# Another order of sections and blocks in z, three products instead of two in attention V, and maxima by transfer

## The chip, the cores and the metric

The kernel runs on one core of a Trainium2 chip. The metric is the device time of one execution in microseconds (us), the median of three runs. A core has TensorE (PE, matrix products, into PSUM), VectorE (DVE), ScalarE (ACT), GpSimd (POOL) and SyncE (SP), which here issues nearly all transfers (DMA). Each engine takes its instructions in a fixed order and waits on semaphores.

## The reference, cut to what matters

Two layers over 2048 latent and 256 context tokens of width 1024. In each, one input projection gives the columns of three head groups: a gMLP with spatial gating inside chunks of 128 (a_u, a_v, a_g), grouped-query attention with 8 heads of 64 and 2 key heads (q, k, v, b_g), and a bidirectional RG-LRU (r_x, r_g). The three results, gated, go through the output projection, a residual and a LayerNorm.

```python
z = (x * (1 + scale[:, None]) + shift[:, None]) @ w_in
a_u, a_v, a_g, q, k, v, b_g, r_x, r_g = jnp.split(z, IN_OFFSETS, -1)
q = axial_rope(rms_norm(q, q_norm_g), rows, cols)      # k likewise
attn = blocked_attention(q, concat([k, kc]), concat([v, vc]))   # softmax over 2304 keys
mix_a = chunk_gmlp(a_u, a_v, a_norm_g, a_norm_b, a_ws, a_bs)
xr = centred_dwconv(r_x, conv_w, conv_b)
lru = h_f + h_b                                        # one scan in each direction
y = concat([mix_a * silu(a_g), attn * silu(b_g), lru * silu(r_g)], -1) @ w_o
x_new = layer_norm(ALPHA * x + gate[:, None] * y, ln_g, ln_b)
```

In the last layer the context tokens need only what the latent tokens read of them (k, v and the LRU's state).

## The kernel before

A layer is a z phase and an attention phase. Both cut the tokens into nine blocks of 256: block 0 is the context, blocks 1 to 8 the latent tokens. Operands are split into a high and a low part in fp16, so that most products are sums of three.

**The z phase** (`z_phase`). A block's input is transposed and modulated by `prep` (PE tr, ACT xm, POOL xh, DVE xl). Then sections are run for the block, each a group of columns of the projection: rx and rg (LRU, products named cps), ag, kv, uv, bg (products named zps), in the order of the tuple `run`. A section's evacuations are ACT and DVE work out of PSUM. Longer follow-ups are generators: `lru` (convolution on DVE up to xrh and xrl, then the gate products gps on PE), `heads` (norm and rope of q and k on DVE and POOL, transposes kp and qp on PE, stores of QS), `gmlp` (products ga, transpose yt). `start` puts one into a list, and each `tick` of a section takes every one on to its next `yield`; so the yields set where a follow-up's PE work stands between the sections. Only PE's order is written out by hand in this phase; the other engines' is set by the scheduler. `rest` (`ada_rest`, the remaining adaLN vectors: products gtp, transposes gtr) and `fm` (`first_max`, the maxima of attention's first unit, products zms) are pumped between products inside a section. The last two blocks are woven by hand. PSUM banks are shared by tags: zc (cps, gps), tr (tr, kp, qp, yt, gtr, zms; two banks), zps (four banks).

**The attention phase** (`att_phase`). A unit is a block and a head, 136 in all (72 and 64). Its keys come in steps of 256: nine steps in a latent unit, one in a context unit, 1160 steps in all. A step has four score products of 256 columns (stp, two for each key tile: KK times QS, then KB times QB), ACT's exponential into P, a subtraction that gives the low part Pl (on POOL, now and then on DVE, by the costs that `use` adds up), and four steps later (LAG) the products with V (`attend`). Row 64 of QB holds the negated maximum of each query, so that the score comes out shifted. That maximum is made two to three units ahead: `max_chunks` (ten score products sps of 512 or 256 columns, reduced by DVE into pm, then mz), paced by `pace`; three steps behind the last chunk `row_out` calls `max_row`. At fixed rates the steps also take along the out-projection (wo: groups of three products wops of 512 columns, 32 groups a block in 17 blocks), its LayerNorm, the backward scan and the loading of weights. The order of PE, DVE, ACT and POOL is written out by hand here; SP's is the scheduler's.

Of the kernel before, what the change touches and what calls it, by code (L numbers as in the profile page):

```python
# [20 lines left out]
KC = 8  # L21
# [34 lines left out]
def tile_hybrid_groups(  # L56
# [23 lines left out]
    MZ = [cst.tile([128, 2, 65], F16, name=f"MZ{i}") for i in range(3)]  # L80
# [6 lines left out]
    def consts_late():  # L87
        V.memset(nhalf, -0.5)
        V.tensor_copy(idH, idF)
        V.memset(VX[:, :, :, 128:129], 1.0)  # L90
        for m in MZ:
            V.memset(m, 0.0)
        G.memset(KB[64:65], 1.0)
# [162 lines left out]
    def layer(l):  # L256
# [15 lines left out]
        def z_phase():  # L272
# [33 lines left out]
            def ada_rest():  # L306
                items = [(l2, j, k) for l2, j in [(0, 2)] + [(a, b) for a in range(1, DEPTH) for b in (2, 1, 0)]
                         for k in range(KC)]
                zer = MZ[1][:, 0, 0:1].to_broadcast([128, 128])
                mov = MZ[2][:, 0:1, 0:64].to_broadcast([128, 4, 64])  # L310
# [7 lines left out]
                def fin(l2, j, row):  # L318
# [13 lines left out]
                for i, (l2, j, k) in enumerate(items):  # L332
                    if k == 0:
                        acc = pp.tile([128, 256], F32, name="gtp", tag="zps", bufs=4)
# [12 lines left out]
                    if k == KC - 1:  # L347
                        V.tensor_tensor(row, acc, row, op=OP.add)
                        fins = l2, j, row
# [11 lines left out]
            def lru(b):  # L361
# [15 lines left out]
                yield  # L377
                rr = zp.tile([128, 2, 2, n], F32, name="gt0", tag="gt0")
# [58 lines left out]
            IW = 1.0 / WS  # L437
            xT = {}
# [13 lines left out]
            def prep(b):  # L452
# [4 lines left out]
                def xload(h):  # L457
                    for t in range(2):
                        xt = zp.tile([128, 512], F32, name="xn", tag="xn", bufs=4 if l == 0 else 2)
                        nc.sync.dma_start(xt, src[t * 128:(t + 1) * 128, h * 512:(h + 1) * 512])  # L460
                        xn[t, h] = xt
# [26 lines left out]
            def nat(xT_b, t, g, c0=0):  # L488
# [5 lines left out]
                for k in range(KC):  # L494
# [3 lines left out]
                    if t:  # L498
                        pump(fm, 1)
# [46 lines left out]
            def heads(b, qk, ss):  # L546
# [50 lines left out]
                yield  # L597
                for t in range(2):
# [20 lines left out]
            def first_max(QS):  # L619
# [11 lines left out]
                V.tensor_reduce(MZ[0][:, :, 64], zm, axis=AX, op=OP.max, negate=True)  # L631

            def sections(b, bi):
# [19 lines left out]
                def sec_rx():  # L653
# [13 lines left out]
                    if b >= 2 and (bi != 2 or full(0)):  # L667
# [3 lines left out]
                def sec_rg():  # L671
                    sg = zp.tile([128, 2, n], F32, name="sg", tag="sbg")
# [19 lines left out]
                def sec_kv():  # L692
                    pump(late, 100)
                    h0 = 0 if full(b) else 8
                    for t in range(2):
# [12 lines left out]
                        tick()  # L708
                    hd.append(heads(b, qk, ss))
# [14 lines left out]
                def sec_bg():  # L724
                    for t in range(2):
                        sbg = zp.tile([128, 512], F32, name="sbg", tag="th" if t and b < NB - 1 and (full(0) or bi != 2) else "sbg")
# [10 lines left out]
            def queue(*bis):  # L737
# [5 lines left out]
                start(chain())  # L743

            border = list(range(NB)) if full(0) else [1, 0] + list(range(2, NB))
            with tc.manual_schedule(engines={nc.tensor.engine}):
# [16 lines left out]
                for bi, b in enumerate(border):  # L763
# [26 lines left out]
        def att_phase():  # L790
# [8 lines left out]
            p = Router(op, ["aQS aQB", "P Pl", "asb wad brow pxn pxm pm ol rc", "yB yt aya ayc", "OH OL",  # L799
# [107 lines left out]
            blk, sbs, yas = {}, {}, {}  # L907
# [20 lines left out]
            def max_chunks(u):  # L928
# [4 lines left out]
                mz = MZ[u % 3]  # L933
                for t in range(2):
                    pm = p.tile([128, 5], F32, name="pm", tag="pm", bufs=4)
                    i = 0
                    for k0 in range(0, nk, 512):
# [8 lines left out]
                        if k0 + 512 >= nk:  # L946
                            V.tensor_reduce(mz[:, t, 64:65], pm[:, :i], axis=AX, op=OP.max, negate=True)
# [3 lines left out]
            def max_row(u):  # L951
                b, h = units[u]
                mz = MZ[u % 3]
# [85 lines left out]
            def attend(u, j):  # L1039
# [3 lines left out]
                if j == 0:  # L1043
                    pvs[u] = pp.tile([128, 2, 130], F32, name="pv", tag="pv" if b else "sps", bufs=2 if b else 3)
# [16 lines left out]
            def head_out(u):  # L1061
                b, h = units[u]
                pv = pvs.pop(u)
                ol = p.tile([128, 2, 64], F32, name="ol", tag="ol", bufs=2)
                S.copy(ol, pv[:, :, 0:64])
                yield
# [5 lines left out]
                V.reciprocal(rc, pv[:, :, 128])  # L1072
                V.tensor_tensor(pv[:, :, 64:128], ol, pv[:, :, 64:128], op=OP.add)
                for t in range(2):
                    hs = slice(h * 64, (h + 1) * 64)
                    V.scalar_tensor_tensor(yB[:, t, hs], pv[:, t, 64:128], rc[:, t:t + 1], sb[:, t, hs],  # L1076
                                           op0=OP.mult, op1=OP.mult)
                use(DV, 0.85)
                if h == 7:
                    outs.append(mix_t(b))  # L1080

# [293 lines left out]
```

## Time and profile before

| | |
|---|---|
| median of 3 runs | 2864.6 us (2861.25 to 2867.11) |
| profiled execution, own time | 2865.65 us |
| its span, first to last instruction | 2863.9 us |
| mean granted TensorE clock | 0.982 of full |
| z of layer 0, attention of layer 0 | about 0 to 664 us, 664 to 1500 us |
| z of layer 1, attention of layer 1 | about 1500 to 2070 us, 2070 to 2864 us |

Everything below is of the profiled execution. The stages overlap a little, and the borders are those of the first and last products of each.

### The profile page before, as it was taken

The numbers are of one execution on the slowest core, as the hardware profiler recorded it, in microseconds if no ns is written. First come the engines' busy times: TensorE is split into PE (matmuls) and PEld (weight loads), VectorE is DVE, ScalarE is ACT, GpSimd is POOL, SyncE is SP. The second block draws the span as 40 slices with busy tenths as digits, with TensorE's granted clock in tenths as the row PEclk, the third lists the DMA queues.
The fourth block names the chain that finished last, engine by engine and source line by source line (L and its number), as shares of the span: only waits on it lengthen the run. The fifth ranks groups of instructions, "written<-read, shape, count | busy, mean of one in ns | idle before, by whom it ended". The sixth has DMA issues, their size and how long they took to land. (4 is left out here: it accounts for less than half of the span.)

```text
span 2863.9 us, 60755 instructions
## 1 busy us (share of the span) xinstructions
PE 2688.2 (94%) x24121; PEld 1816.1 (63%) x24121; DVE 2031.8 (71%) x4013; ACT 1341.6 (47%) x2513; POOL 1757.0 (61%) x1812
## 2 busy tenths in 40 slices
PE   7999999889999998999999999998899999999998
PEld 3555555546776776677764655564487777777775
DVE  5565554558998876777887565554699898777776
ACT  2444343345654444444543454444466454454442
POOL 3244443346987876677864244443499897777774
PEclk9999999999999999999999999999999999999999
DMA  8232222105222210211115111110322321111001
GB/s 292 87 103 94 87 91 83 58 35 175 68 83 87 77 42 24 75 49 53 49 53 161 53 60 52 52 65 36 121 76 72 93 93 38 49 53 39 30 31 45
DMA packets 113717, 213.61 MB, mean 75 GB/s; under 512 B 13396, under 2 KB 45016, under 8 KB 113432
## 3 DMA queue, kind: packets, MB, share of 16 engines
q1 hardware_dynamic: 111060, 208.84, 21.9%
q8 instruction: 189, 3.10, 0.5%
q10 hardware_dynamic: 2372, 0.89, 0.1%
q14 instruction: 96, 0.79, 0.1%
HBM read 147.54 MB, written 62.14 MB: 73 GB/s over the span
## 5 line engine op out<-in xcount | busy, mean ns | idle before, releaser
L1036 POOL TENSOR_TENSOR Pl<-P 128x512 f16<-128x512 f32 x1118 | 1197.8, 1089 | 310.9 <-ACT P L1029 304.9
L1029 ACT ACTIVATE P<-stp 128x512 f32<-128x512 f32 x1160 | 692.0, 598 | 754.9 <-PE stp L1026 713.2
L942 DVE TENSOR_REDUCE pm<-sps 128x1 f32<-128x256 f32 (+1 forms) x1276 | 777.1, 628 | 249.8 <-PE sps L940 246.5
L1026 PE MATMUL stp<-aQB,KB 65*128 65x256 f16 x2320 | 579.6, 275 | 2.7 <-ACT aQB L957 2.7
L1025 PE MATMUL stp<-aQS,KK 128*128 128x256 f16 x2320 | 577.4, 274 | 0.2
L1053 PE MATMUL pv<-VX,P 128*128 128x129 f16 x4640 | 557.7, 220 | 1.3 <-ACT aQB L957 0.8
L1055 PE MATMUL pv<-VX,Pl 128*128 128x65 f16 x4640 | 527.3, 193 | 1.5 <-POOL Pl L1036 0.9
L1055 PEld LDWEIGHTS <-Pl 128*128 128x128 f16 x4640 | 414.9, 97 | 121.6 <-POOL Pl L1036 3.2
L940 PE MATMUL sps<-KK,aQS 128*128 128x256 f16 (+1 forms) x1276 | 456.3, 359 | 36.6 <-DVE pm L942 26.7
L1053 PEld LDWEIGHTS <-P 128*128 128x128 bf16 x4640 | 430.4, 98 | 41.5 <-issue 25.4
L1025 PEld LDWEIGHTS <-KK 128*128 128x128 f16 x2320 | 229.6, 99 | 85.8 <-issue 21.9
L1026 PEld LDWEIGHTS <-KB 65*128 65x128 f16 x2320 | 227.8, 98 | 70.5 <-issue 1.3
L484 POOL TENSOR_SCALAR xh<-xm 128x512 f16<-128x512 f32 x68 | 44.6, 656 | 288.3 <-ACT xm L481 287.7
L495 PEld LDWEIGHTS <-xh 128*128 128x128 f16 x1040 | 102.5, 99 | 122.9 <-issue 17.8
L497 PEld LDWEIGHTS <-xl 128*128 128x128 f16 x1040 | 102.4, 98 | 123.1 <-issue 3.5
L496 PEld LDWEIGHTS <-xh 128*128 128x128 f16 x1040 | 102.5, 99 | 115.6 <-issue 9.5
L646 PE MATMUL cps<-xh,wh_cc 128*128 128x256 f16 x528 | 148.7, 282 | 3.3 <-POOL xh L484 2.9
L648 PE MATMUL cps<-xh,wl_cc 128*128 128x256 f16 x528 | 148.1, 280 | 3.3 <-DVE wl_cc L158 3.3
L647 PE MATMUL cps<-xl,wh_cc 128*128 128x256 f16 x528 | 148.4, 281 | 0.4 <-DVE xl L485 0.4
L940 PEld LDWEIGHTS <-aQS 128*128 128x128 f16 x1276 | 125.1, 98 | 16.8 <-issue 2.1
L397 POOL TENSOR_SCALAR gt<-gt,sp 128x256 f32<-128x256 f32 x72 | 43.9, 618 | 144.8 <-ACT gt L394 138.8
L719 ACT ACTIVATE uv<-uv 128x512 f32<-128x512 f32 x34 | 21.4, 630 | 208.0 <-DVE uv L718 208.0
(273 smaller groups left out, 5416.2 us busy)
## 6 DMA issues: line engine op xcount, KB each, us to landing
wf<-in_w_in_dram SPq DMA_DIRECT2D x64, 256.0 KB
wga<-in_w_ada_dram SPq DMA_DIRECT2D x32, 512.0 KB
lr<-LRd SPq DMA_DIRECT2D x32, 512.0 KB
SBd<-sbg SPq DMA_DIRECT2D x34, 256.0 KB
QSd<-QS SPq DMA_DIRECT2D x17, 512.0 KB
LRd<-gt SPq DMA_DIRECT2D x34, 256.0 KB
aQS<-QSd SPq DMA_DIRECT2D x17, 512.0 KB
asb<-SBd SPq DMA_DIRECT2D x17, 512.0 KB
```

The costliest lines, as they stand in the source:

```text
L495: T.matmul(ps[:, :w], xh[:, k, ts], wh[:, k, c0:], start=(k == 0), stop=False)
L646: T.matmul(ps, wh[:, k, cs], xh[:, k], start=(k == 0), stop=False)
L647: T.matmul(ps, wh[:, k, cs], xl[:, k], start=False, stop=False)
L648: T.matmul(ps, wl[:, k, cs], xh[:, k], start=False, stop=(k == KC - 1))
L940: T.matmul(ps[:, :w], QS[:, h, t * 128:(t + 1) * 128], KK[:, kv].rearrange("p a b -> p (a b)")[:, k0:k0 + w], start=True, stop=True)
L942: V.tensor_reduce(pm[:, i:i + 1], ps[:, :w], axis=AX, op=OP.max)
L1025: T.matmul(ps[:, i], KK[:, kv, kt], QS[:, h], start=True, stop=False)
L1026: T.matmul(ps[:, i], KB[:, kv, kt], QB[:, h], start=False, stop=True)
L1029: S.activation(P, ps, AF.Exp)
L1036: less_busy(0.8, 1.06, 0.8).tensor_tensor(Pl, P, Ph, op=OP.subtract)
L1053: T.matmul(pv[:, t, 0:129], Ph[:, i, ts], VX[:, kt, kv, 0:129], start=first, stop=False, skip_group_check=True)
L1055: T.matmul(pv[:, t, 64:129], Pl[:, i, ts], VX[:, kt, kv, 64:129], start=False, stop=end, skip_group_check=True)
```

## The change

In z:
- layer 0 runs bg ahead of uv; block 7 runs three sections (rx, rg, ag) in its own turn instead of four, and the last two blocks are woven as rx 8, kv 7, uv 7, ag 8, kv 8, bg 7, uv 8, rg 8, bg 8;
- lru of blocks 7 and 8 starts in that block's kv, ahead of its heads, instead of in the next block's rx (block 7) or behind kv and heads (block 8); lru has one more yield in layer 0 (blocks up to 6), heads one more in all blocks but the last;
- sg and the first sbg of block 8 are taken from tag xn, both sbg of block 7 from tag sbg; the last prep is led two steps forward; first_max is pumped in both halves of a section;
- the gtr transposes write the free part of gtp's bank instead of a bank of tag tr.

In attention:
- the product with the high part of P, 129 columns, becomes two of 65 and 64, so that V's two halves sum up in the same 65 columns of PSUM with the low part's product; the copy to ol and the addition of the halves go;
- the maximum goes from mz (128 partitions) into row 64 of QB by two transfers, where two products (mp) and a copy on ACT did it. `MZ`, its zeros and its use as a zero operand go; `zeros` takes the last.

```diff
-                        tp = pp.tile([128, KC, 2], F32, name="gtr", tag="tr", bufs=2)
...
-                        acc = pp.tile([128, 256], F32, name="gtp", tag="zps", bufs=4)
+                        bank = pp.tile([128, 512], F32, name="gtp", tag="zps", bufs=4)
+                        acc = bank[:, 0:256]
...
                 yield
                 yield
+                if l == 0 and b < NB - 2:
+                    yield
                 rr = zp.tile([128, 2, 2, n], F32, name="gt0", tag="gt0")
...
-                    if t:
-                        pump(fm, 1)
+                    pump(fm, 1)
...
-                    if b >= 2 and (bi != 2 or full(0)):
+                    if 2 <= b < NB - 1 and (bi != 2 or full(0)):
                         start(lru(b - 1))
...
-                    sg = zp.tile([128, 2, n], F32, name="sg", tag="sbg")
+                    sg = zp.tile([128, 2, n], F32, name="sg", tag="xn" if b == NB - 1 else "sbg", bufs=xb if b == NB - 1 else None)
...
+                    if b >= NB - 2:
+                        start(lru(b))
                     hd.append(heads(b, qk, ss))
...
+                    if l == 0:
+                        run = ("rx", "rg", "ag", "kv", "bg", "uv")
                     if bi == NB - 2:
-                        run = run[:4]
+                        run = run[:3]
...
-                for f in (sec["rx"], prv["uv"], sec["ag"], sec["kv"]):
-                    f()
-                start(lru(NB - 1))
-                for f in (sec["uv"], prv["bg"], sec["rg"], sec["bg"]):
+                for f in (sec["rx"], prv["kv"], prv["uv"], sec["ag"], sec["kv"], prv["bg"],
+                          sec["uv"], sec["rg"], sec["bg"]):
                     f()
...
             def max_row(u):
                 b, h = units[u]
-                mz = MZ[u % 3]
-                mp = pp.tile([65, TB], F32, name="mp", tag="sps", bufs=3)
+                mz = mzs.pop(u, mz0)
                 for t in range(2):
-                    T.matmul(mp[:, t * 128:(t + 1) * 128], mz[:, t], idH, start=True, stop=True)
-                S.copy(blk[b][1][64:65, h], mp[64:65])
+                    nc.sync.dma_start(blk[b][1][64:65, h, t * 128:(t + 1) * 128], mz[:, t:t + 1])
...
-                        T.matmul(pv[:, t, 0:129], Ph[:, i, ts], VX[:, kt, kv, 0:129], start=first,
+                        T.matmul(pv[:, t, 0:65], Ph[:, i, ts], VX[:, kt, kv, 64:129], start=first,
                                  stop=False, skip_group_check=True)
-                        T.matmul(pv[:, t, 64:129], Pl[:, i, ts], VX[:, kt, kv, 64:129], start=False,
+                        T.matmul(pv[:, t, 0:64], Ph[:, i, ts], VX[:, kt, kv, 0:64], start=False,
+                                 stop=False, skip_group_check=True)
+                        T.matmul(pv[:, t, 0:65], Pl[:, i, ts], VX[:, kt, kv, 64:129], start=False,
                                  stop=end, skip_group_check=True)
...
-                V.tensor_tensor(pv[:, :, 64:128], ol, pv[:, :, 64:128], op=OP.add)
```

What the scheduler and the written order make of it stands here for three engines. First VectorE in the tail of layer 0's z phase, before, around the evacuations of block 8's rx; t, kc and qc are the rope work of heads 7, xr, xrh and xrl the convolution of lru 7:

```order
L661 COPY rx<-rx 128x2
L578 TENSOR_TENSOR t_5424<-qk_4994,ct 128x512
L578 TENSOR_TENSOR t_5424<-qk_4994,ct 128x128
L370 SCALAR_TENSOR_TENSOR xr<-rx,pc,xr 128x256
L586 TENSOR_TENSOR t_5424<-t_5424,t_5431 128x640
L370 SCALAR_TENSOR_TENSOR xr<-rx,pc,xr 128x256
L588 CAST kc<-t_5424 128x2x128
L593 CAST qc<-t_5424 128x8x64
L589 TENSOR_TENSOR kc<-t_5424,kc 128x2x64
L594 TENSOR_TENSOR qc<-t_5424,qc 128x8x64
L373 CAST xrh<-xr 128x512
L375 TENSOR_TENSOR xrl<-xr,xrh 128x512
```

And now, around the evacuations of block 7's kv (VX, ss):

```order
L366 TENSOR_SCALAR xr<-rx,pc 128x256 x2
L370 SCALAR_TENSOR_TENSOR xr<-rx,pc,xr 128x256 x4
L419 SCALAR_TENSOR_TENSOR gt_5203<-lra,hc,gt_5204 128x256 x2
L370 SCALAR_TENSOR_TENSOR xr<-rx,pc,xr 128x256
L422 COPY hc<-gt_5203 128x2
L370 SCALAR_TENSOR_TENSOR xr<-rx,pc,xr 128x256
L707 SCALAR_TENSOR_TENSOR VX<-zps,VX 128x2x64
L373 CAST xrh<-xr 128x512
L711 TENSOR_REDUCE ss<-sq 128x10
L375 TENSOR_TENSOR xrl<-xr,xrh 128x512
L562 TENSOR_TENSOR qk_4973<-qk_4973,rs 128x640
```

The convolution of lru 7 stood behind both halves of the rope work and stands ahead of its first operation now.

Next TensorE in one step of attention, before: a chunk product and the pair that is repeated four times a step:

```order
L940 LDWEIGHTS aQS
L940 MATMUL sps<-KK,aQS 128x512
L1053 LDWEIGHTS P
L1053 MATMUL pv<-VX,P 128x129
L1055 LDWEIGHTS Pl
L1055 MATMUL pv<-VX,Pl 128x65
```

And now:

```order
L951 LDWEIGHTS aQS
L951 MATMUL sps<-KK,aQS 128x512
L1062 LDWEIGHTS P
L1062 MATMUL pv<-VX,P 128x65
L1064 LDWEIGHTS P
L1064 MATMUL pv<-VX,P 128x64
L1066 LDWEIGHTS Pl
L1066 MATMUL pv<-VX,Pl 128x65
```

Each pair has become three products, and P is loaded as weights once more.

Last SyncE at the start of layer 0's attention, before (lr: the backward scan's input, wof: rows of w_o):

```order
L826 DMA lr<-LRd_8_295 128x4x256
L873 DMA wof<-in_w_o_dram 128x1024 x2
L826 DMA lr<-LRd_7_294 128x4x256
L873 DMA wof<-in_w_o_dram 128x1024
L911 DMA aQS<-QSd_6_257 128x2048
L913 DMA aQB<-QSd_6_257 64x2048
```

And now, where aQB<-mz is half a unit's row of maxima:

```order
L837 DMA lr<-LRd_8_292 128x4x256
L966 DMA aQB<-mz 1x128x1 x2
L884 DMA wof<-in_w_o_dram 128x1024
L966 DMA aQB<-mz 1x128x1 x2
L884 DMA wof<-in_w_o_dram 128x1024
L966 DMA aQB<-mz 1x128x1
L837 DMA lr<-LRd_7_291 128x4x256
L966 DMA aQB<-mz 1x128x1 x3
```

The rows stand between the large loads of the same queue.

## Rows read from the trace of the kernel before

**Rows 1.** The page's first part: busy time, share of the span, instructions.

```profile
PE 2688.2 (94%) x24121; PEld 1816.1 (63%) x24121; DVE 2031.8 (71%) x4013; ACT 1341.6 (47%) x2513; POOL 1757.0 (61%) x1812
```

**Rows 2.** Stage windows: start:end, length, busy us (instructions), granted clock, DMA share, GB/s.

```profile
434.00:444.20 10.20, 8.28 (x34) 4.96 (x35) 3.70 (x10) 2.54 (x5) 5.52 (x7) 0.50 0.07 27
560.00:664.00 104.00, 88.06 (x504) 47.43 (x503) 64.12 (x117) 44.11 (x76) 45.03 (x50) 0.94 0.22 75
664.00:940.00 276.00, 259.90 (x2995) 203.38 (x2996) 249.88 (x487) 154.43 (x290) 241.64 (x232) 0.98 0.29 94
1960.00:2070.00 110.00, 91.12 (x531) 49.58 (x530) 70.20 (x128) 48.31 (x83) 48.40 (x52) 0.94 0.22 74
```

**Rows 3.** TensorE's waits, 60 to 560 us: total us, times, longest.

```profile
PE zps L495 <- DVE uv L720: 6.2, 5, 1.2
PE gtr L322 <- ACT KB L608: 4.7, 1, 4.7
```

**Rows 4.** TensorE's waits in layer 0's tail, 560 to 664 us.

```profile
PE gps L386 <- DVE xrh L373: 5.6, 1, 5.6
PE gps L386 <- DVE sg L676: 3.0, 1, 3.0
PE cps L646 <- POOL xh L484: 2.9, 1, 2.9
PE zms L629 <- DVE zm L630: 2.3, 4, 1.6
...
PE zms L629 <- DVE ya L543: 1.7, 1, 1.7
```

**Rows 5.** TensorE's waits in layer 1's tail, 1960 to 2070 us.

```profile
PE gps L386 <- DVE xrh L373: 10.3, 1, 10.3
...
PE gps L387 <- DVE xrl L375: 1.5, 1, 1.5
```

**Rows 6.** TensorE's timeline in three steps of one attention unit.

```profile
1002.28 0.27 PE L1025 MATMUL stp<-aQS,KK 128*128 128x256 f16 x1
...
1002.95 0.22 PE L1053 MATMUL pv<-VX,P 128*128 128x129 f16 x1
1003.00 0.19 PE L1055 MATMUL pv<-VX,Pl 128*128 128x65 f16 x1
1003.03 0.22 PE L1053 MATMUL pv<-VX,P 128*128 128x129 f16 x1
...
1003.29 0.27 PE L1025 MATMUL stp<-aQS,KK 128*128 128x256 f16 x1
...
1005.40 0.28 PE L956 MATMUL mp<-idH,MZ 128*65 128x128 f16 x2
1005.51 0.38 PE L940 MATMUL sps<-KK,aQS 128*128 128x512 f16 x1
...
1007.95 0.28 PE L1026 MATMUL stp<-aQB,KB 65*128 65x256 f16 x1
```

**Rows 7.** VectorE's timeline in the same unit.

```profile
1001.40 0.16 DVE L947 TENSOR_REDUCE MZ<-pm 128x1 f16<-128x5 f32 x1
```

**Rows 8.** Lines 957 (aQB) and 940 (sps): waits in us, times.

```profile
  PE sps L940: 7.3, 15
  PE stp L1026: 2.7, 8
...
  DVE pm L942: 26.7, 48
```

**Rows 9.** The additions of V's halves: ns min/median/max, first and last start.

```profile
L1073 DVE TENSOR_TENSOR pv<-ol,pv x136: 295/295/297, 683.1 to 2830.0; 128x128 f32<-128x128 f32 x136
```

**Rows 10.** SyncE: a wait on loads, and one line's issues.

```profile
SPq L569 <- DMA rp<-in_rope_dram: 17.9, 14, 1.6
...
L839 SPq DMA_DIRECT2D YCd<-yc x34: 513/525/1193, 750.4 to 2354.8; - x34
```

**Rows 11.** Window of the densest stretch of products in attention.

```profile
1084.71:1088.11 3.40, 3.40 (x56) 3.19 (x53) 2.50 (x12) 2.61 (x6) 2.90 (x3) 1.00 0.02 5
```

More of the change, by code (lines that the diff above doesn't have):

```diff
@@ L79, in tile_hybrid_groups @@
     VX = cst.tile([128, NKT, 2, 130], F16, name="VX")
-    MZ = [cst.tile([128, 2, 65], F16, name=f"MZ{i}") for i in range(3)]
+    zeros = cst.tile([128, 192], F16, name="zeros")
+    mz0 = cst.tile([128, 2], F16, name="mz0")
     def rsq(pool, dst, src, scale, eps, n):
@@ L90, in consts_late @@
         V.memset(VX[:, :, :, 128:129], 1.0)
-        for m in MZ:
-            V.memset(m, 0.0)
+        V.memset(zeros, 0.0)
         G.memset(KB[64:65], 1.0)
@@ L308, in ada_rest @@
                          for k in range(KC)]
-                zer = MZ[1][:, 0, 0:1].to_broadcast([128, 128])
-                mov = MZ[2][:, 0:1, 0:64].to_broadcast([128, 4, 64])
+                zer = zeros[:, 0:128]
+                mov = zeros[:, None, 128:192].to_broadcast([128, 4, 64])
                 ws, acc, row, fins = [], None, None, None
@@ L316, in ld, with fin @@
                     nc.sync.dma_start(ws[-1], w_ada[l2, k * 128:(k + 1) * 128, j * D:(j + 1) * D])
-                def fin(l2, j, row):
+                def fin(l2, j, row, tp):
                     if j < 2:
-                        tp = pp.tile([128, KC, 2], F32, name="gtr", tag="tr", bufs=2)
                         for k in range(KC):
@@ L348, in ada_rest @@
                         V.tensor_tensor(row, acc, row, op=OP.add)
-                        fins = l2, j, row
+                        fins = l2, j, row, bank[:, 256:256 + 2 * KC].rearrange("p (k i) -> p k i", i=2)
                     for _ in range(4):
@@ L437, in z_phase @@
             IW = 1.0 / WS
+            xb = 4 if l == 0 else 2
             xT = {}
@@ L458, in xload @@
                     for t in range(2):
-                        xt = zp.tile([128, 512], F32, name="xn", tag="xn", bufs=4 if l == 0 else 2)
+                        xt = zp.tile([128, 512], F32, name="xn", tag="xn", bufs=xb)
                         nc.sync.dma_start(xt, src[t * 128:(t + 1) * 128, h * 512:(h + 1) * 512])
@@ L597, in heads @@
                 yield
+                if b < NB - 1:
+                    yield
                 for t in range(2):
@@ L725, in sec_bg @@
                     for t in range(2):
-                        sbg = zp.tile([128, 512], F32, name="sbg", tag="th" if t and b < NB - 1 and (full(0) or bi != 2) else "sbg")
+                        g = "xn" if b == NB - 1 and not t else "th" if t and b < NB - 2 and (full(0) or bi != 2) else "sbg"
+                        sbg = zp.tile([128, 512], F32, name="sbg", tag=g, bufs=xb if g == "xn" else None)
                         ps = nat(xTb, t, "bg")
@@ L742, in queue @@
                 queued.update(border[i] for i in bis)
-                start(chain())
+                g = chain()
+                start(g)
+                if bis[-1] == NB - 1:
+                    for _ in range(2):
+                        next(g, 0)
             border = list(range(NB)) if full(0) else [1, 0] + list(range(2, NB))
@@ L797, in pop @@
                 return st.enter_context(tc.tile_pool(name=f"aps{l}_{i}", bufs=1, space=PSUM, reuse_waits="tile"))
-            p = Router(op, ["aQS aQB", "P Pl", "asb wad brow pxn pxm pm ol rc", "yB yt aya ayc", "OH OL",
+            p = Router(op, ["aQS aQB", "P Pl", "asb wad brow pxn pxm pm mz rc", "yB yt aya ayc", "OH OL",
                             "gB lng lnb r xw st6 amv arv rsq1"])
@@ L932, in max_chunks @@
                 nk = CTX + SEQ if b else CTX
-                mz = MZ[u % 3]
+                mz = mzs[u] = p.tile([128, 2], F16, name="mz", tag="mz", bufs=6)
                 for t in range(2):
@@ L1043, in attend @@
                 if j == 0:
-                    pvs[u] = pp.tile([128, 2, 130], F32, name="pv", tag="pv" if b else "sps", bufs=2 if b else 3)
+                    pvs[u] = pp.tile([128, 2, 66], F32, name="pv", tag="pv" if b else "sps", bufs=2 if b else 3)
                 pv = pvs[u]
@@ L1063, in head_out @@
                 pv = pvs.pop(u)
-                ol = p.tile([128, 2, 64], F32, name="ol", tag="ol", bufs=2)
-                S.copy(ol, pv[:, :, 0:64])
-                yield
                 sb = sbs[b]
@@ L1071, in head_out @@
                 rc = p.tile([128, 2], F32, name="rc", tag="rc", bufs=2)
-                V.reciprocal(rc, pv[:, :, 128])
-                V.tensor_tensor(pv[:, :, 64:128], ol, pv[:, :, 64:128], op=OP.add)
+                V.reciprocal(rc, pv[:, :, 64])
                 for t in range(2):
                     hs = slice(h * 64, (h + 1) * 64)
-                    V.scalar_tensor_tensor(yB[:, t, hs], pv[:, t, 64:128], rc[:, t:t + 1], sb[:, t, hs],
+                    V.scalar_tensor_tensor(yB[:, t, hs], pv[:, t, 0:64], rc[:, t:t + 1], sb[:, t, hs],
                                            op0=OP.mult, op1=OP.mult)
-                use(DV, 0.85)
+                use(DV, 0.6)
                 if h == 7:
                     outs.append(mix_t(b))
+                yield
             def mix_t(b):
```

7 lines of the change are left out of this document (3 added, 4 removed).

## The prediction

> **What bounds the kernel now.** I read the page first: TensorE is busy for 94% of the span [rows 1], so a gain must come from its idle time, its slow clock, or work it no longer does. The stage windows then show where it is not full: at the end of the z phase of both layers, in 560 to 664 us and 1960 to 2070 us, it is busy 88.06 of 104 and 91.12 of 110 us, at a mean granted clock of 0.94. In the first 276 us of attention VectorE and GpSimd are as full as TensorE (249.88, 241.64 and 259.90 us) [rows 2]. Last come the waits of TensorE, by stretch. In the tails one wait is the longest: the first gate product (gps) waits for xrh, 5.6 us in layer 0 and 10.3 in layer 1 [rows 4, 5]. VectorE's order, shown with the change, says why: ahead of xrh stands the whole rope work of block 7. So the z phase has some 50 us that order can give back, and attention is bound by TensorE's own work with some waits on VectorE.
>
> **The z phase, part by part.** Each term is a wait that the new order no longer makes.
> 1. In layer 0, bg now comes ahead of uv. Today bg's second half waits for a PSUM bank that uv's long evacuation holds: 6.2 us in 5 waits [rows 3]. After uv now comes rx of the next block, which takes another tag (zc). Gain 6.2.
> 2. The transposes of the adaLN row (gtr) no longer ask for a "tr" bank, which waits 4.7 us behind the copy of KB [rows 3]; they use the free half of their own accumulator's bank. Behind that wait the engine stands at its lower level: clock 0.50 from 434 to 444.2 us [rows 2], that is 10.2 us at 1.2 instead of 2.4 GHz, 5.1 us of work. Gain 9.8.
> 3. Tail of layer 0. lru(7) now starts behind kv of block 7 and ahead of heads(7), and kv(7), uv(7) stand between it and its first gps. VectorE's order has xrh ahead of the rope work now. TensorE has the 10 us of uv(7) to do meanwhile; what VectorE must do first is some ten operations under 1 us each. So 5.6 goes. The 3.0 us behind sg goes too: sg of block 8 gets a buffer of its own tag (xn) instead of waiting for the store of the last sbg. The ten products of the first maxima (zms) are spread over both halves of the last bg instead of one, so that their two waits, 2.3 and 1.7, go [rows 4]. Gain 12.6.
> 4. Tail of layer 1, the same: 10.3 and 1.5 for xrh and xrl [rows 5], and 3.0 for sg, as in layer 0 [rows 4]. Gain 14.8.
> 5. Clock: 0.06 of 104 and of 110 us is 12.8 us of work lost in the tails [rows 2]. It fell behind the long waits; where 2.9 us of waiting for xh stays (rx(8) keeps its place behind the last transposes) [rows 4], some of it stays. I take half, 6.
>
> Together 49.4. Against it: VectorE keeps its work (64.12 of 104 us in the tail [rows 2]), and lru(8), heads(8) and the evacuation of bg now follow each other; in layer 1 the later kp and qp stand directly ahead of tr, all three in two banks. New waits there are bounded by nothing below, and above by the whole 49.4. I take a third, 16.4, since the deepest stalls came from one misplaced chain. **z: -33.**
>
> The rest I cost at nothing: heads one tick later spares kp its short waits for kc, and lru one tick later moves products that wait for nothing now; the zeros tile replaces three memsets before the start; sbg and sg in other buffers are freed by stores 10 us ahead of their next use; the two early steps of the last prep only move loads forward, on SP, which waits there for others anyway.
>
> **Attention, part by part.**
> 6. The two products that turned the maxima into a row (mp) go: 1005.40 to 1005.51 us, 0.11 for both [rows 6], 136 times: 15.0.
> 7. mp shared the three banks of the score chunks and was freed by ScalarE's copy; TensorE waited for that copy 7.3 us (chunks) and 2.7 us (scores) [rows 8]. Gain 10.
> 8. A pair of products becomes three, with the same 194 columns: 65, 64 and 65, and one more weight load. Four pairs take 1002.95 to 1003.29, 0.085 us each; a product of 65 columns lets the next start 0.03 us later, with a weight load behind it [rows 6]. So the new load fits behind a short product as the old ones do, and three short products take 0.0875 to 0.09: 2.5 to 5 ns more, 4640 times, 12 to 23 us. I take 12, since the columns alone are equal; below, nothing.
> 9. VectorE loses the addition (295 ns, 136 times: 40 us) [rows 9], ScalarE two copies. Chunk products wait 26.7 us for VectorE in all [rows 8]; the engine is near its limit only in the first third of each attention phase, so about 45 of the 136 units, and 45 x 0.295 = 13 us of its work lie in the way. GpSimd is as full there, and its work stays. I take 6 of 0 to 13.
> 10. The row now goes by 272 transfers of 128 elements of two bytes. No such transfer is in the trace. Nearest rows: a load of 64 KB makes SP's next transfer wait up to 1.6 us behind its issue, and a transfer of 256 short pieces takes 0.53 us to issue [rows 10]; so 2.1 us from issue to landing, and I allow 2.5. How early is it? In a usual unit the maximum is ready at 1001.56, and the first product that reads the row starts at 1007.95 [rows 6, 7]: 6.4 us, which was hidden so far by holding mp back for three steps. SP need not hold back. So the row lands 4 us early; only where 512 KB loads are queued ahead can it be late. SP's order shows rows mixed with such loads, but by the program those ahead of a row wait for work that stands ahead of the row's own maximum. I take +5, bounds 0 and 40.
>
> **Attention: -15.0 - 10 + 12 - 6 + 5 = -14.**
>
> **Sum.** The profiled execution took 2865.65 us (span 2863.9 and 1.75 around it), 1 us above the median of the runs. 2865.65 - 33 - 14 = 2818.7; against the median that is 2817.6. I say **2818**.
>
> **Rivals.**
> *The idle time only moves* (chance 0.15). If VectorE's work in the tails sets their length, another product waits for it: lru(8), heads(8) and the gate chain of block 7 all fall between kv(8) and the last transposes. For: VectorE is 62% busy there, and busiest exactly there. Against: TensorE has 104 us of work and VectorE 64. Then terms 3 to 5 give nothing, the rest stays: 16 - 5 + 14 = 25 below, 2841.
>
> *TensorE cannot start products that fast* (chance 0.10). A step without out-projection has 13 products now, and takes 1002.28 to 1003.29 us, 1.01 us [rows 6] or 78 ns each; it would have 17 in the same time, 59 ns. The densest stretch of the trace, 3.4 us at 1084.71, ran 56 products, 61 ns each, with no idle time [rows 11]; nothing here is denser for longer. If about 62 ns were a floor, such a step would take 17 x 0.062 = 1.054 us, 0.045 more. Of the 1160 steps (128 units of nine, 8 of one) 544 carry three long products of the out-projection (17 blocks of 32) and have room; 616 x 0.045 = 28 us. Time: 2818 + 28 = 2846. The Trainium skill ("TensorE: Matmul & The Clock Gate", section "Wait — 56ns, not 53.3ns?") says that with hardware decoding off the sequencer spends about 62 ns on each matmul, and that this is the bound once the array work is shorter. In a short burst the trace is below that, 43 ns a product over the eight of [rows 6], as a queue behind the sequencer would allow; over a whole step nothing here is below 61, so the trace doesn't exclude it, and by that rule this rival's time is the right one.
>
> *The row comes late* (chance 0.12): slower. SP issues in order, and it is parked for long: a row that stands behind a transfer whose data come late, or behind loads on the same rings, holds the scores of its unit, and with them every engine. Each microsecond of mean lateness costs 136 us. It decides from 47 / 136 = 0.35 us of mean lateness on; with half the units 1.5 us late the time is 2865 + 55 = 2920. For: where a unit starts before its row's three steps are over (`upto`, around the context heads) there is less slack, and a row in elements is unlike any transfer of the trace. Against: 4 us of slack in the usual unit. The Trainium skill ("DMA: Bandwidth & Descriptors", section "Specifications") says that transfers in pieces below 512 B are done by read-modify-write; no run here shows what that costs.
>
> Something else in a change of this many parts: 0.05.
>
> **How the numbers follow.** The forecast has 0.58; its own range, with new waits between 5 and 30 us and term 8 between 0 and 23, is 2800 to 2838. The range must leave out no more than 2 in 10: forecast, first and second rival hold 0.83, and reach from 2792 (no new wait, no late row, the third product nearly free) to 2858. A difference below 0.2%, 5.7 us, cannot be told from no change. Faster: the forecast, nearly all of the first two rivals and a little of the rest, 0.82. Slower: the third rival, 0.12. Same: 0.06.
>
> **What would show it.** In the changed profile: no wait of gps for xrh above 1 us in either tail, no gtr wait, no zps wait for uv; the clock of both tails above 0.97; three pv products in 0.0875 us; no wait of stp for aQB beyond a few us in sum. I am wrong if stp waits for a transfer in many units, if the pv products stand 60 ns apart, or if kp, qp and gps of block 8 wait as long as xrh did before.

## The result and the profile after

The changed kernel takes 2833.07 us (median of 4 runs, 2831.34 to 2834.73) against 2863.14 us of the kernel before, a ratio of 0.9888 (95% interval 0.9873 to 0.9902; the two medians alone give 0.9895): 1.1% faster, inside the range, and 15 us above the time that I named. The profiled execution took 2831.34 us. Its busy times, against [rows 1]:

```profile
PE 2679.1 (95%) x28489; PEld 1813.1 (64%) x28489; DVE 2002.0 (71%) x3874; ACT 1271.2 (45%) x2242; POOL 1770.3 (63%) x1813
```

TensorE has 18% more recorded instructions and is busy for 9 us less. The four phases, each cut at the first and the last score product of a layer (columns as in [rows 2]), first before, then after:

```profile
0.00:664.30 664.30, 600.85 (x3785) 334.69 (x3786) 364.43 (x699) 271.45 (x501) 247.04 (x288) 0.96 0.32 108
664.30:1483.60 819.30, 784.23 (x8583) 590.70 (x8581) 675.42 (x1379) 416.32 (x794) 641.35 (x630) 0.99 0.20 64
1483.60:2069.70 586.10, 533.84 (x3260) 311.08 (x3258) 352.99 (x651) 256.44 (x475) 231.96 (x272) 0.97 0.21 73
2069.70:2826.10 756.40, 740.87 (x8336) 565.49 (x8335) 616.48 (x1249) 395.37 (x740) 630.29 (x614) 1.00 0.18 58
```

```profile
0.00:639.40 639.40, 593.30 (x3779) 331.96 (x3779) 364.75 (x691) 271.10 (x501) 248.01 (x288) 0.97 0.32 109
639.40:1449.50 810.10, 780.89 (x10764) 588.39 (x10762) 660.06 (x1324) 379.98 (x653) 651.57 (x631) 0.99 0.23 68
1449.50:2029.90 580.40, 533.09 (x3271) 312.72 (x3269) 345.73 (x633) 254.02 (x472) 231.09 (x273) 0.97 0.21 71
2029.90:2791.90 762.00, 743.48 (x10499) 565.77 (x10497) 609.96 (x1192) 364.19 (x615) 633.26 (x614) 1.00 0.20 60
```

The z phases fell by 24.9 and 5.7 us, attention by 9.2 in layer 0, and in layer 1 it rose by 5.6. Both attention phases got the same edits, so something in them seems to pay in one and to cost in the other; one profile on each side can't show that, and the experiments come back to it. Next the 6.8 us near half speed that are left of the 10.2, and the two tails of z, which [rows 2] show at 0.94; layer 0's is no better now:

```profile
420.50:427.30 6.80, 5.08 (x20) 1.55 (x20) 5.34 (x13) 0.63 (x1) 0.00 (x0) 0.54 0.49 157
535.00:639.40 104.40, 90.04 (x492) 47.39 (x490) 68.19 (x122) 48.07 (x82) 47.02 (x52) 0.93 0.17 60
...
1920.00:2029.90 109.90, 95.44 (x531) 49.75 (x528) 70.32 (x126) 50.89 (x87) 46.58 (x52) 0.97 0.18 62
```

And TensorE's waits there, for 60 to 535 us, for the tail of layer 0 and for that of layer 1 [rows 3 to 5]:

```profile
PE gtp L335 <- DVE sbg L736: 4.7, 1, 4.7
...
PE gps L388 <- DVE sg L680: 4.4, 1, 4.4
PE gps L388 <- ACT gt L394: 3.5, 1, 3.5
...
PE gps L389 <- DVE xrl L375: 4.5, 1, 4.5
PE gps L388 <- DVE sg L680: 4.3, 1, 4.3
```

The 6.2 us of zps for uv are gone, and the waits for xrh too. But gtr's 4.7 us came back as 4.7 us of gtp, with the half clock behind it, sg is waited for longer than before (3.0 us in both tails), and gps now waits for ScalarE's gt and for xrl. In attention a triple of products now takes 0.09 us; four of them start at 1001.14 and the next work at 1001.50:

```profile
1001.14 0.19 PE L1062 MATMUL pv<-VX,P 128*128 128x65 f16 x1
1001.17 0.19 PE L1064 MATMUL pv<-VX,P 128*128 128x64 f16 x1
1001.20 0.19 PE L1066 MATMUL pv<-VX,Pl 128*128 128x65 f16 x1
1001.23 0.19 PE L1062 MATMUL pv<-VX,P 128*128 128x65 f16 x1
...
1001.50 0.38 PE L1154 MATMUL wops<-OH,ayc 128*128 128x512 f16 x1
```

That is 5 ns more than a pair took [rows 6], by the rounded starts; over all undisturbed pairs and triples of layer 0's attention the means are 86.7 and 91.0 ns. The rows by transfer, by their line, and TensorE's two waits that they bear on (48 waits for pm, 26.7 us, before [rows 8]):

```profile
L966 SPq DMA_DIRECT2D aQB<-mz x272: 468/469/1224, 636.7 to 2777.7; - x136
...
PE stp L1035 <- DMA aQB<-mz: 16.9, 13, 3.2
PE sps L951 <- DVE pm L953: 12.1, 23, 3.1
```

### The profile page after: what moved, and what is told of

Read it like the earlier page. It is cut to its first block, busy times and chain, and to the rows that moved or that the text cites. A ratio compares the mean times of both kernels' runs of the same rounds, so it can differ in the third digit from the quotient of the medians.

```text
span 2829.5 us, 69703 instructions
## 1 busy us (share of the span) xinstructions
PE 2679.1 (95%) x28489; PEld 1813.1 (64%) x28489; DVE 2002.0 (71%) x3874; ACT 1271.2 (45%) x2242; POOL 1770.3 (63%) x1813
## 5 line engine op out<-in xcount | busy, mean ns | idle before, releaser
L1035 PE MATMUL stp<-aQB,KB 65*128 65x256 f16 x2320 | 580.1, 274 | 17.1 <-DMA aQB<-mz 16.9
L1066 PE MATMUL pv<-VX,Pl 128*128 128x65 f16 x4640 | 543.4, 194 | 6.5 <-POOL Pl L1045 6.1
L1062 PE MATMUL pv<-VX,P 128*128 128x65 f16 x4640 | 541.0, 192 | 2.2 <-DVE pm L953 2.2
L1064 PE MATMUL pv<-VX,P 128*128 128x64 f16 x4640 | 540.5, 192 | 0.0
L1064 PEld LDWEIGHTS <-P 128*128 128x128 bf16 x4640 | 429.9, 97 | 118.8 <-issue 4.4
L951 PE MATMUL sps<-KK,aQS 128*128 128x256 f16 (+1 forms) x1276 | 456.3, 359 | 13.7 <-DVE pm L953 12.1
L1062 PEld LDWEIGHTS <-P 128*128 128x128 bf16 x4640 | 439.3, 98 | 30.1 <-issue 13.5
L1066 PEld LDWEIGHTS <-Pl 128*128 128x128 f16 x4640 | 428.8, 97 | 7.9 <-POOL Pl L1045 7.5
L498 PEld LDWEIGHTS <-xh 128*128 128x128 f16 x1040 | 102.6, 99 | 123.8 <-issue 16.9
```

The lines of the kernel that those rows point to most:

```text
L951: T.matmul(ps[:, :w], QS[:, h, t * 128:(t + 1) * 128], KK[:, kv].rearrange("p a b -> p (a b)")[:, k0:k0 + w], start=True, stop=True)
L1035: T.matmul(ps[:, i], KB[:, kv, kt], QB[:, h], start=False, stop=True)
L1062: T.matmul(pv[:, t, 0:65], Ph[:, i, ts], VX[:, kt, kv, 64:129], start=first, stop=False, skip_group_check=True)
L1064: T.matmul(pv[:, t, 0:64], Ph[:, i, ts], VX[:, kt, kv, 0:64], start=False, stop=False, skip_group_check=True)
L1066: T.matmul(pv[:, t, 0:65], Pl[:, i, ts], VX[:, kt, kv, 64:129], start=False, stop=end, skip_group_check=True)
```

## The experiments

All ratios are to the kernel before, run on the same chip; the changed kernel has 0.9888.

**The two parts alone.** z's part without attention's, and attention's without z's, as the section on the change lists them.

> The z part of the change alone, attention as before. By the two traces z fell by 24.9 us in layer 0 and 5.7 us in layer 1, 30.6 in all, so the theory that the parts simply add says 2863 - 30.6 = 2832.5 (2828 to 2837). Rival: attention's part is a hidden loss, so that z alone is faster than the whole change, 2825 or less. Second rival: my forecast's 14 us for attention is there but something at the border of the phases eats it, then z alone stands at 2845.

Measured: 2850.66 us, ratio 0.9936 (0.9923 to 0.995), 18 us of gain. Against the 2863 from which the expectations count, that ratio is 2845, the number of the second rival: z's part alone gives 18 us, and attention's part some 14 on top of it. That a border eats the 14 us elsewhere, as the rival has it, is not shown. In its profile layer 0's z takes 642.1 us, but layer 1's 587.1:

```profile
1465.40:2052.50 587.10, 540.80 (x3259) 316.79 (x3257) 353.18 (x650) 254.50 (x474) 229.42 (x272) 0.96 0.21 72
```

So the 5.7 us of layer 1's z do not show with z's order alone. But TensorE's waits there, all rows of the view summed, fell as in the changed kernel (51.9 us before, 45.8 here), and the clock of 0.96 instead of 0.97 is 6 us of work; one profile does not tell whose the 5.7 us are.

> The attention part alone, z as before. If the parts add: 2863 - 3.6 = 2859.5 (2855 to 2863), since by the traces the first attention phase fell by 9.2 us and the second rose by 5.6. Rival, the forecast's terms: -14, 2849.

Measured: 2860.75 us, 0.9978 (0.9968 to 0.9987), 6 us of gain; against 2863 that is 2857, inside the first expectation. The parts give 25 us one by one and 32 together. The 7 us between have an uncertainty of about 6 (the three intervals, added in squares), so whether the parts help each other stays open. On top of the other, z's part is worth 0.9888/0.9978, 26 us, and attention's 0.9888/0.9936, 14 us.

**Two products and the addition back.** The product of 129 columns, ol's copy and the addition as before; rows still by transfer.

```diff
-T.matmul(pv[:, t, 0:65], Ph[:, i, ts], VX[:, kt, kv, 64:129], ...)
-T.matmul(pv[:, t, 0:64], Ph[:, i, ts], VX[:, kt, kv, 0:64], ...)
-T.matmul(pv[:, t, 0:65], Pl[:, i, ts], VX[:, kt, kv, 64:129], ...)
+T.matmul(pv[:, t, 0:129], Ph[:, i, ts], VX[:, kt, kv, 0:129], ...)
+T.matmul(pv[:, t, 64:129], Pl[:, i, ts], VX[:, kt, kv, 64:129], ...)
```

> The changed kernel with V's halves summed as before (products of 129 and 65 columns, the copy and the addition are back), the row still by transfer. Theory: the third product costs about 4.4 ns each of 4640 times by the spacing of starts, 20 us, against which the addition of 295 ns loads VectorE in the first third of each phase, up to 14.6 us of chunk waits: 2833 - 20 + 5 = 2818 (2813 to 2828). Rival: the third product is nearly free and the lost addition was the gain: 2839 to 2846.

Measured: 2836.88 us, 0.9891 (0.9876 to 0.9906), no difference; neither expectation was right. Its attention phases and its wait for VectorE:

```profile
642.70:1463.70 821.00, 779.54 (x8446) 582.49 (x8444) 680.25 (x1385) 389.70 (x724) 640.35 (x630) 0.98 0.23 67
...
2045.80:2801.40 755.60, 736.25 (x8215) 558.39 (x8213) 620.01 (x1255) 372.78 (x678) 629.25 (x615) 0.99 0.21 60
...
PE sps L951 <- DVE pm L953: 28.4, 49, 3.0
```

Attention of layer 0 is 10.9 us slower than with three products, that of layer 1 is 6.4 us faster. By the spacing of starts two products instead of three save 10 us in each layer, as expected. What the addition costs was not: the chunk waits rise from 12.1 to 28.4 us, by 10.9 in layer 0 and 5.4 in layer 1. In layer 0 that only balances the cheaper pair; most of the rest is the clock, 0.98 here and 0.99 in the changed kernel, some 8 us of work, and one profile does not tell whether the waits brought that about. The experiment with three products in layer 0 alone, further down, settles it by whole runs.

**The row by products again.** The two products (mp) and the copy are back, three products with V stay.

> The changed kernel with the row of maxima made by two products and a copy as before; three products with V stay. Theory: the two products and the wait behind them stood for 31 us of TensorE's time, the late rows for 17 us now, so the row by products costs 14 us more: 2847 (2840 to 2852). Rival: the transfer is a net loss, since it is late at 15 units and parks SyncE: 2826 or less.

Measured: 2847.52 us, 0.9928 (0.9916 to 0.9941), 11.5 us slower than the changed kernel. The theory holds: the transfer is a gain, net of its late rows.

**Heads without the extra yield in layer 1.**

```diff
-                if b < NB - 1:
+                if b < NB - 1 if l == 0 else b == NB - 2:
                     yield
```

> The changed kernel without the extra yield of heads in layer 1's blocks 1 to 6 (block 7 and layer 0 keep it). In the changed kernel the products ga of layer 1 wait 3.1 us at a time for vhl, in three blocks, and in two of them the granted clock falls to half right behind; before, the same blocks waited 0.7 to 1.4 us three times for kc and KB, and the clock stayed full. Theory (one long wait costs the clock, three short ones don't): the idle time stays about as it is, 9 us, and 2 or 3 stretches at half clock go, 3 to 5 us: 0.9888 becomes 0.987 to 0.988, about 2829. Rival: the wait only moves and the clock does not care where: 2833. Second rival: the yield was a gain after all, and kp's waits come back with more than 10 us: 2838.

Measured: 2831.95 us, 0.9874 (0.986 to 0.9888): 4 us in the expected direction, but the intervals meet, so a gain is not shown. The profiles show what the edit does in three blocks of layer 1, first of the changed kernel, with its 3.4 us behind one of the waits and the wait itself, then of this one:

```profile
1692.90:1887.60 194.70, 181.17 (x1113) 106.98 (x1111) 106.51 (x201) 88.04 (x165) 77.80 (x92) 0.98 0.15 55
...
1703.40:1706.80 3.40, 3.40 (x18) 2.41 (x16) 2.95 (x9) 0.00 (x0) 0.00 (x0) 0.51 0.58 231
...
PE ga L530 <- POOL vhl L522: 8.8, 3, 2.9
```

```profile
1703.20:1765.70 62.50, 59.56 (x372) 34.86 (x370) 34.55 (x65) 28.52 (x55) 25.55 (x31) 1.00 0.16 57
1765.70:1828.20 62.50, 59.56 (x372) 34.87 (x370) 34.55 (x65) 28.52 (x55) 25.55 (x31) 1.00 0.16 58
1828.20:1891.80 63.60, 60.25 (x376) 35.38 (x374) 34.96 (x67) 29.63 (x57) 26.19 (x31) 1.00 0.16 57
```

Behind that wait of 2.9 us the engine stands at 1.2 GHz for 3.4 us; here, with several waits of 0.4 to 1.2 us a block and about the same sum, it stays at 2.4 GHz. Over the whole of layer 1's z little is left of it: 579.4 us here, 580.4 in the changed kernel.

**Three products in layer 0, two in layer 1.** The two forms of the experiment above, chosen by `last`.

> The changed kernel with three products with V in layer 0 and two (and the addition) in layer 1. Theory: the split pays where VectorE is as full as TensorE and loses where it isn't. Of the four kernels so far, two products against three cost 10.9 and 4.6 us in the first attention phase and gain 6.4 and 8.9 us in the second; so 6 to 9 us below the changed kernel, 2825 (ratio 0.986). Rival: the two effects are of the clock's scatter, no difference, 2833.

Measured: 2824.13 us, 0.9849 (0.9835 to 0.9864). The theory holds; it gave 11 us. The experiment with two products in both layers (0.9891) differs from this one in layer 0 alone, so three products there are worth 0.0042, 12 us. Both signs are thus shown by whole runs, each size within some 6 us.

**What a third product is made of.** The product with V's low half has 32 columns; half of the low part is left out.

```diff
-T.matmul(pv[:, t, 0:64], Ph[:, i, ts], VX[:, kt, kv, 0:64], ...)
+T.matmul(pv[:, t, 0:32], Ph[:, i, ts], VX[:, kt, kv, 0:32], ...)
```

> The changed kernel with the product of P and V's low half cut from 64 to 32 columns (half of V's low part is left out). It asks what a third product is made of. If columns set the distance of starts, the cut product lets the next start 13.3 ns sooner, 4640 times 13.3 ns = 62 us of TensorE's work less, and the time falls to 2775 to 2800. If a floor for each product (its weight load or its issue) of about 28 to 30 ns sets it, nothing changes: 2828 to 2836. With a floor of 62 ns a product, as my rival had it, also nothing.

Measured: 2822.61 us in one run. TensorE's timeline:

```profile
1001.07 0.19 PE L1062 MATMUL pv<-VX,P 128*128 128x65 f16 x1
1001.10 0.18 PE L1064 MATMUL pv<-VX,P 128*128 128x32 f16 x1
1001.13 0.19 PE L1066 MATMUL pv<-VX,Pl 128*128 128x65 f16 x1
1001.16 0.19 PE L1062 MATMUL pv<-VX,P 128*128 128x65 f16 x1
```

Neither expectation is right as it stands. The 32 columns are 13.3 ns at 2.4 GHz, and the next start is 27 ns behind (median), where behind 64 columns it was 28. So there is a floor. But the start behind the last of the three fell from 33 to 29 ns, 5 or 6 ns a triple in all, which is some 25 us of starts. The time is some 10 us shorter, by a single run.

**The row on ScalarE's queue**, and one step behind the last chunk instead of three.

```diff
-nc.sync.dma_start(blk[b][1][64:65, h, ...], mz[:, t:t + 1])
+nc.scalar.dma_start(blk[b][1][64:65, h, ...], mz[:, t:t + 1])
...
-rows.append([u, 3])
+rows.append([u, 1])
```

> The changed kernel with the rows of maxima issued by ScalarE (its own queue), one step behind the last chunk, instead of by SyncE. In the changed kernel 15 units wait for their row, 17 to 19 us in all; in 4 of them SyncE issued it 2 to 4.5 us behind its maximum, in most others it landed 3.5 to 4.5 us behind its issue instead of 2.8. Theory (the queue shared with large loads makes it late): waits for rows fall below 8 us, 2820 to 2827. Rival: the issue, 0.47 us twice a unit by SyncE's rows, stands in ScalarE's way ahead of the exponentials, 128 us of its time in all, and TensorE waits for P or stp instead: 2840 or more.

Measured: 2934.12 us, 1.0232 (1.0218 to 1.0246): 100 us slower than the changed kernel. The rival's price is there, by another way. The wait for the row is the one that grew, by 76 of the 100 us; the clock of the two attention phases, 0.97 and 0.98, covers the rest:

```profile
  PE stp L1035: 93.3, 54
```

ScalarE issues in its own order: the second half of a row goes out a median of 2.1 us behind the end of its maximum, the one step of delay included; SyncE, which is parked for the row, did so a median of 0.03 us behind it. Nor did a queue without the large loads bring a row faster: from issue to landing the first halves took a median of 2.8 us, as on SyncE's, and the second 3.7. This is what my third rival would have looked like.

**The first row of a phase by products**, all others by transfer.

> The changed kernel, with the row of each phase's first unit alone made by two products and a copy, as before; all others stay transfers. Theory: at the two borders the row's 2.8 us and more stand on the path with nothing beside them (stp waits 1.6 and 3.4 us), and behind the second the clock falls; two products and a copy take some 0.9 us each. So 3 to 8 us less than the changed kernel: 2826 to 2830 (ratio 0.987). Rival: the first unit is held by its chunk maxima and VectorE anyway, no difference: 2833 (0.9888).

Measured: 2832.88 us, 0.9889 (0.9872 to 0.9907), no difference, the rival's number. The row's wait at the border into layer 1's attention (3.2 us) is gone. What stands there now is the wait for the last gMLP block's sag, which the changed kernel has too, and one for the copy:

```profile
2027.96 0.95 PE L543 MATMUL yt<-idF,sag 128*128 128x128 f32 x4 [1.26 <-DVE sag L536]
...
2030.03 0.27 PE L1042 MATMUL stp<-aQB,KB 65*128 65x256 f16 x1 [0.90 <-ACT aQB L969]
```

**Maxima one step earlier**, so that rows have about 1 us more.

```diff
-rate = max(rate, (need[u] - pumped) / max(begin[u] - 5 - s, 1))
+rate = max(rate, (need[u] - pumped) / max(begin[u] - 6 - s, 1))
```

> The changed kernel with the pace of the maxima set to be done six steps ahead of a unit instead of five. One step is 1.0 to 1.1 us. Theory: late rows cost their wait; of the 13 waits beyond the borders, 14.5 us in sum, seven are under 1 us and go, the six others lose 1 us each: 9 to 10 us less waiting, and 5 to 10 us less time, 2823 to 2828 (ratio 0.985 to 0.987). Rival: VectorE can't make the maxima earlier where it is full, the chunk products wait instead, and the time stays: 2833.

Measured: 2823.73 us, 0.9854 (0.9839 to 0.9868), 10 us faster than the changed kernel and inside the expectation. In its profile the waits for rows fall from 13 to 7 and from 16.9 to 12.1 us only. Attention of layer 0 takes 803.1 us, with the clock at 1.00:

```profile
639.10:1442.20 803.10, 777.79 (x10765) 586.45 (x10763) 659.31 (x1328) 378.69 (x653) 650.23 (x629) 1.00 0.23 69
```

The changed kernel has 810.1 there, but the next experiment, which leaves that phase alone, has 806.5. So where half of the gain comes from stays open.

**gtr in its old bank.** `tp` is taken from tag tr again, and gtp is a bank of its own.

> The changed kernel with the gtr transposes back in a bank of tag tr. In the changed kernel the 4.7 us wait of gtr for KB is gone, but the next gtp product waits 4.7 us for a bank that sbg's evacuation holds, and the clock falls behind it as it did before. Theory: VectorE is late at that place (rope work and the scan in front of sbg), whichever bank is asked for, so nothing changes: 2833 (0.988 to 0.9895). Rival: the half bank that gtr now holds is what makes the fourth bank short; then the old bank removes the wait and the half clock: 2825 (0.986). Second rival, the forecast's term: 10 us slower, 2843.

Measured: 2828.65 us, 0.9866 (0.9849 to 0.9883): 6 us faster, though the intervals still meet. The profiles bear the rival out: the longest wait at that place is 2.3 us, the clock stays full where the changed kernel has 0.54, and layer 0's z takes 635.2 us (635.1 with the four edits together, below), against 639.0 to 643.2 in the ten profiles that have the new order of z without this edit.

```profile
0.00:635.20 635.20, 591.53 (x3779) 332.01 (x3779) 366.49 (x691) 270.94 (x501) 248.64 (x288) 0.98 0.32 110
420.00:430.00 10.00, 7.74 (x66) 5.86 (x65) 8.05 (x19) 3.55 (x7) 1.03 (x1) 1.00 0.36 112
...
PE qp L616 <- DVE adaT L324: 2.3, 1, 2.3
```

**The last four edits with a lower time, together.** These are three products in layer 0 only, no extra yield of heads in layer 1, maxima one step earlier, and gtr in its old bank.

> The changed kernel with the four edits that helped: three products with V in layer 0 and two in layer 1, no extra yield of heads in layer 1's blocks 1 to 6, maxima one step earlier, gtr in its old bank. Measured one by one against the changed kernel's ratio of 0.9888 they gave 0.0039, 0.0014, 0.0034 and 0.0022. Theory (they sit in different stages and add): 0.9888 - 0.0109 = 0.978, about 2803 (2798 to 2810). Rival: some of these were scatter of the clock, or the early maxima and VectorE's additions in layer 1 stand in each other's way: 2812 to 2820 (0.981 to 0.984).

Measured: 2808.52 us (2805.88 to 2810.59), 0.9797 (0.9776 to 0.9818), against 0.978 as the sum; the edge of the rival, 0.981, lies inside the interval too. It is the fastest version here, 0.9% below the changed kernel.

## Why the prediction was right, and where its steps were not

The sign, the range and the two main mechanisms held: z lost idle time, and attention lost the row products. The size was 47 us and is 30 to 32.

Of z's 33 us, 18 are there with z's part alone and 26 on top of attention's. In layer 0's z TensorE's waits, all rows of the view summed, fell from 63.2 to 45.7 us, and a clock of 0.97 instead of 0.96 is 7 us of work; together that is about the 24.9 us. Attention's part gives 6 us alone and 14 on top of z's. That 14 was also the forecast is in part luck: its row was 8 us too good and its third product with the addition 6 us too dear. The sum of the forecast is right. Its own range is narrower than its two terms at their ends give (2795 to 2843), on which nothing hangs here.

**Term 1 held** by the trace, with no run of its own: no wait of zps for uv is left. A gain that I did not price came beside it: three waits of gtp for its loads, in the view of [rows 3], are gone as well.

```profile
PE gtp L343 <- DMA wga<-in_w_ada_dram: 8.3, 3, 2.8
```

**Term 2 failed in sign.** I took away gtr's wait for a bank and forgot what the half bank then holds: gtp's bank stays taken until gtr is done, and the next gtp needs the fourth bank, which waits for VectorE's sbg. The forecast had 9.8 us for it; taking it back gains 6 us by the medians and 4 by layer 0's z. The new order alone, with the old bank, has no wait of gtr for KB left.

**Terms 3 and 4 were oversized, and one of their rows was read by half.** The waits of the two tails, all rows of their views summed, fell from 18.0 to 14.3 and from 18.8 to 14.5 us, by 3.7 and 4.3 instead of 12.6 and 14.8. The 16.4 us that I set against all terms cover most of that, by luck, since I took a third of the sum and worked it out from no row. The row read by half is sg's. I took it for a wait for an SBUF buffer. What gps waits for is a PSUM bank that it shares with cps, free only when VectorE has made sg. Before, ScalarE's step of sg did wait for the store of the last sbg, for 0.91 of the 3.0 us (0.89 in layer 1):

```profile
643.10 0.38 ACT L675 ACTIVATE sg<-cps 128x256 f32<-128x256 f32 x1 [0.91 <-DMA SBd<-sbg]
```

The new buffer took that away, and now VectorE decides. VectorE in the tail of layer 0 after the change, and the product that waits:

```profile
622.63 0.69 DVE L523 TENSOR_TENSOR vhl<-uv,vhl 128x512 f16<-128x512 f32 x1 [3.43 <-POOL vhl L522]
623.24 0.41 DVE L680 SCALAR_TENSOR_TENSOR sg<-sg,cps 128x256 f32<-128x256 f32 x1
...
623.71 0.27 PE L388 MATMUL gps<-xrh,lwh 128*128 128x256 f16 x1 [4.35 <-DVE sg L680]
```

VectorE stands 3.43 us for GpSimd's vhl with sg queued behind it. A new buffer cannot help there.

**Term 5**, the clock of the tails, had 6 us. Layer 0's went from 0.94 to 0.93, and layer 1's from 0.94 to 0.97, which is 3 us of work. My sign, above 0.97 in both, did not come.

**"Heads one tick later" was no pure gain.** I costed it at nothing. In three blocks of layer 1 it spared kp its waits and gave ga one long wait in their place, with the clock behind it in two of them. That the kernel is slower for it is not shown: taking it back moved the time by 4 us, inside the noise, and layer 1's z by 1.

**Terms 6, 7 and 10**, the row: -20 by the forecast, -11.5 by the experiment. The mechanism is right, the lateness was undersized: 16.9 us of waits instead of 5. A row lands a median of 2.8 us behind its issue, where I allowed 2.5, and is issued late at its worst places. Seen in one unit, on SyncE, VectorE and TensorE:

```profile
794.47 0.33 SPq L1131 DMA_DIRECT2D xt<-in_x_dram  x1
800.92 0.38 SPq L837 DMA_DIRECT2D lr<-LRd  x1
801.40 0.54 SPq L850 DMA_DIRECT2D YCd<-yc  x1
802.00 0.61 SPq L966 DMA_DIRECT2D aQB<-mz  x1
...
SPq L837 <- POOL hb L861: 6.0, 1, 6.0
...
797.30 0.16 DVE L958 TENSOR_REDUCE mz<-pm 128x1 f16<-128x5 f32 x1
...
806.14 0.37 PE L1035 MATMUL stp<-aQB,KB 65*128 65x256 f16 x1 [2.19 <-DMA aQB<-mz]
```

The maximum is ready at 797.46, SyncE is parked 6 us for GpSimd's hb, and the row goes out 4.5 us late. I had written that what stands ahead of a row waits only for older work; it does, but older work is not always done sooner. That is the third rival at 16.9 / 136 = 0.12 us a unit, below the 0.35 from which it would have decided.

**Terms 8 and 9**, the third product and the addition. By the starts the product costs 20 us (4.3 ns, 4640 times), where I took 12 of 12 to 23. The addition and the copy are worth about as much, not 6, since taking both edits back changes nothing, to within some 6 us. My step took only the first third of each phase and half of that; without the edit the waits for VectorE came back in both layers, twice as long in layer 0. That three products pay in layer 0 and cost in layer 1 is shown; that these waits alone decide it is not, since in layer 0 the clock fell with them.

**The rivals.** The idle time did move in part (term 2, the tails). The second is refuted: the densest stretch, counted as in [rows 11], now has 72 products in 3.4 us, 47 ns each, and the products with V start 28 to 33 ns apart.

```profile
2785.76:2789.16 3.40, 3.40 (x72) 3.18 (x70) 3.09 (x7) 2.39 (x4) 3.17 (x4) 1.00 0.20 77
```

The Trainium skill ("TensorE: Matmul & The Clock Gate", section "Wait — 56ns, not 53.3ns?") has beside its 62 ns for decoding off another rule: start to start never drops below about 25 ns, however few the columns. The 27 ns behind 32 columns agree with that rule. Starts 28 ns apart, thousands of times, leave no room for 62 ns each.

## What to carry to other kernels

A wait has to be followed to what really releases it, a PSUM bank or a buffer, and to what is queued ahead of the releaser; an edit that frees one bank by holding another only moves the wait. An edit that trades one engine's work for another's is decided stage by stage: here the same edit gained some 11 us in one layer and lost 6 to 11 in the other, and a choice by layer got 11 us that the whole kernel's time had hidden. A small transfer that hides in the mean still has to hide at its worst place: one more step of slack came with 10 us, half of which the waits show, and a queue whose engine has other work cost 100. And a phase of one profile moves by several us with the clock alone, so a gain of that size needs whole runs.

## What the runs showed of the hardware

A product of 32 columns lets the next start after 27 ns, one of 64 or 65 after 28 to 29, and the last in a row of three such products, each with its own weight load, after 33 (29 where the middle one had 32 columns). At 2.4 GHz 32 columns would be 13.3 ns, so the columns alone do not set that distance; whether the load or the issue does is open. One wait of 2.9 us was followed by 3.4 us at 1.2 GHz in two of three blocks; several waits of 0.4 to 1.2 us in the same blocks left the clock at 2.4 GHz. A transfer of 128 pieces of two bytes took 0.47 us to issue and a median of 2.8 us from issue to landing, 4.1 us or more in one of ten.
